# Two closing barriers moved from the end of a log-sum-exp kernel to its beginning

## Chip, cores, metric

One core of a Trainium2 chip. The metric is device time in microseconds (us) of one execution, median of several. All executions quoted here are fast, at a granted clock of 1.00. In the profile DVE is VectorE, ACT ScalarE, POOL GpSimd, SP SyncE and PE TensorE; a q behind a name is that engine's sequencer, and L196 is line 196 of the kernel. The span runs from the program's first instruction to its last.

## The reference

```python
x: float32 [32, 512, 1024], axis = -1
x_max = np.max(x, axis=axis, keepdims=True)
return x_max.squeeze(axis) + np.log(np.sum(np.exp(x - x_max), axis=axis))
```

The kernel reads 67.1 MB, writes 64 KB, and takes the exponentials without subtracting the maximum.

## The kernel before

The 16,384 rows lie as 128 partitions of 128 rows of 1024 numbers. SyncE issues 17 loads of 1 to 16 rows a partition into a ring of 51 rows; ScalarE takes exponentials (and some sums), VectorE the other sums, ScalarE the logarithms, SyncE stores. The parts that matter here:

```python
hook = nc.pop_inst_callback()            # the helper stops recording: what follows is placed by hand
...
body = nc.main_func.blocks[-1]
...
load(0)
n_early = len(body.instructions)         # load 0: will be put ahead of the opening barrier
nc.scalar.preload_act_table_set("natural_log_exp_and_others")
for i, (r, n_dve, parts, by_halves) in enumerate(CHUNKS):
    if i:
        load(i)                          # waits, from load 4 on, for ring rows to be free
    ...                                  # wait for landed[i], exponentials, sums
take_logs(late_row, NB, late[:, : NB - late_row], dves, acts)
nc.sync.wait_ge(act_done, acts)
nc.sync.dma_start(out=out_v, in_=res).then_inc(stored, 16)
nc.sync.sem_clear(range(used[0], used[-1] + 1))
...                                      # load 0 ahead of the opening barrier, the rest right behind it
tc.close()                               # emits the two closing barriers (all five engines)
tc.compile()
nc.sync.wait_ge(stored, 16)              # the program ends when the store has landed
nc.sync.sem_inc(stored, -16)
```

A barrier here works like this in the instruction records: each of the other four engines counts up a semaphore and waits; GpSimd waits for all four counts and then releases the four. The opening barrier stands ahead of the kernel's own code, the two closing ones behind it.

The softmax here doesn't subtract the row's maximum and nothing guards it: scores larger than these inputs give would overflow.

## Time and profile before

| kernel before | |
|---|---|
| time, first 3 runs | 162.74 us (162.58 to 162.85) |
| span of the profiled run | 161.2 us |
| DMA queue, share of 16 engines | 97.3% |
| DVE / ACT busy | 75% / 71% |
| first load issued / landed | 0.00 / 7.6 us |
| second load issued / landed | 0.78 / 25.8 us |
| last load landed / store issued / store landed | 158.2 / 159.6 / 161.2 us |

The timed figure is 1.3 us longer than the span; the runtime's own closing rounds lie behind the span in the semaphore records. The profile's lines stand in the prediction.

### The profile page before, as it was taken

The page shows a single profiled execution, that of the slowest core. Times are in us where ns is not written, and L with a number is a line of the kernel's source. Part 1 is how long each engine was busy: PE and PEld are TensorE (multiplying, and loading weights), DVE is VectorE, ACT ScalarE, POOL GpSimd, SP SyncE. Part 2 cuts the span into 40 slices and gives each one's busy share as a digit, 9 for nine tenths or more (in the row PEclk, how much of TensorE's full clock was granted, in tenths as well). Part 3 has the DMA queues.
Part 4 walks back from the last instruction along what each step waited for, and adds up shares of the span by engine and source line. Part 5 has one row for each costly group of instructions (what it writes and reads, how often), then busy time and mean ns, then how long its engine had stood idle before and what let it go on. Part 6 is the DMA issues. An engine that isn't in the chain of part 4 may idle for free.

```text
span 161.2 us, 149 instructions
## 1 busy us (share of the span) xinstructions
DVE 121.0 (75%) x46; ACT 115.1 (71%) x40; POOL 0.2 (0%) x4
## 2 busy tenths in 40 slices
DVE  0028000003999999999999699999999999999892
ACT  3170005996079960999419993999199999999995
POOL 0000000000000000000000000000000000000000
DMA  7999799999999999999979999999899999999991
GB/s 248 516 488 442 320 457 520 390 390 520 390 390 520 390 390 520 390 390 520 407 342 455 455 455 439 423 423 423 376 439 439 427 448 403 432 415 421 410 409 34
DMA packets 2592, 67.18 MB, mean 417 GB/s; under 512 B 288, under 2 KB 416, under 8 KB 928
## 3 DMA queue, kind: packets, MB, share of 16 engines
q1 hardware_dynamic: 2592, 67.18, 97.3%
HBM read 67.11 MB, written 0.07 MB: 417 GB/s over the span
## 4 chain that ended last, share of the span: by engine, by line
DMA 49%; DVE 29%; ACT 20%; issue 0%
DMA ring<-in_x_dram 49%; DVE sums L154 29%; ACT ring L134 17%; ACT ring L161 3%; ACT res L105 0%
## 5 line engine op out<-in xcount | busy, mean ns | idle before, releaser
L154 DVE TENSOR_REDUCE sums<-ring 128x8 f32<-128x8192 f32 (+5 forms) x14 | 111.2, 7994 | 37.1 <-ACT ring L134 37.0
L134 ACT ACTIVATE ring<-ring 128x8192 f32<-128x8192 f32 (+6 forms) x18 | 104.4, 5835 | 43.7 <-DMA ring<-in_x_dram 43.6
L141 DVE CUSTOM_DVE_ANT_0 ring<-ring 128x512 f32<-128x512 f32 x16 | 9.9, 687 | 0.0
L161 ACT ACTIVATE ring<-ring 128x1024 f32<-128x1024 f32 x9 | 9.3, 1041 | 0.0
L119 ACT ACT_TABLE_LOAD x1 | 1.3, 1283 | 0.8 <-PEq L215 0.8
L161 ACT ACTIVATION_READ_ACCUMULATOR ring<-ring 128x1 f32 x9 | 1.6, 173 | 0.0
L141 DVE DVE_READ_ACCUMULATOR2_ANT sums<- 128x1 f32 x16 | 1.3, 83 | 0.0
L105 ACT ACTIVATE res<-sums 128x81 f32<-128x81 f32 (+1 forms) x2 | 0.5, 246 | 0.0
L105 ACT ACTIVATE res<-late 128x4 f32<-128x4 f32 x1 | 0.2, 173 | 0.0
L215 POOL MEMSET const-bfloat16-1.0<- 128x1 bf16 x1 | 0.1, 102 | 0.0
L215 POOL MEMSET const-uint8-127<- 128x1 uint8 x1 | 0.1, 102 | 0.0
L215 POOL MEMSET const-float32-0.0<- 128x1 f32 x1 | 0.1, 99 | 0.2 <-issue 0.2
L215 POOL MEMSET const-float32-1.0<- 128x1 f32 x1 | 0.1, 99 | 0.0
## 6 DMA issues: line engine op xcount, KB each, us to landing
ring<-in_x_dram SPq DMA_DIRECT2D x1, 7680.0 KB, 25.0
ring<-in_x_dram SPq DMA_DIRECT2D x1, 7168.0 KB, 28.6
ring<-in_x_dram SPq DMA_DIRECT2D x1, 6656.0 KB, 35.7
ring<-in_x_dram SPq DMA_DIRECT2D x1, 4608.0 KB, 20.2
ring<-in_x_dram SPq DMA_DIRECT2D x2, 2048.0 KB, 16.2
ring<-in_x_dram SPq DMA_DIRECT2D x1, 3584.0 KB, 28.3
ring<-in_x_dram SPq DMA_DIRECT2D x1, 2560.0 KB, 27.3
ring<-in_x_dram SPq DMA_DIRECT2D x4, 512.0 KB, 27.0
```

The source lines that it names most:

```text
L105: nc.scalar.activation(out=res[:, lo:hi], in_=src, func=Ln).then_inc(act_done, 1)
L119: nc.scalar.preload_act_table_set("natural_log_exp_and_others")
L134: nc.scalar.activation(out=ring[:, s + lo : s + hi], in_=ring[:, s + lo : s + hi], func=Exp).then_inc(act_done, 1)
L141: nc.vector.tensor_tensor_reduce(out=ring[:, s + j, : D // 2], in0=ring[:, s + j, : D // 2], in1=ring[:, s + j, D // 2 :], scale=1.0, scal ...
L154: nc.vector.reduce_sum(out=sums[:, row + lo : row + hi], in_=ring[:, s + lo : s + hi], axis=AX).then_inc(dve_done, 1)
L161: nc.scalar.activation(out=ring[:, s + j], in_=ring[:, s + j], func=Exp, accum_out=total(row + j),).then_inc(act_done, 1)
L215: nc = _bacc.Bacc("TRN2", target_bir_lowering=False, num_devices=1)
```

## The change

Its intent is to take the two barriers off the end, where they follow the work, and put them at the beginning, where the first load is already under way. The helper is closed at once, so that its barriers are the first thing in the body; all the work comes behind them, and SyncE's wait for the store is the last instruction.

```diff
-    hook = nc.pop_inst_callback()
+    tc.close()
+    tc.compile()
     symbolic, nc._always_lower_symbolic_ap = nc._always_lower_symbolic_ap, False
...
     body = nc.main_func.blocks[-1]
-    assert not body.instructions
+    n_barrier = len(body.instructions)
     load(0)
...
     nc.sync.sem_clear(range(used[0], used[-1] + 1))
+    nc.sync.wait_ge(stored, 16)
+    nc.sync.sem_inc(stored, -16)
...
-    first.instructions = head + work[n_early:] + tail
-    body.instructions = []
+    first.instructions = head
+    body.instructions = work[:n_barrier] + work[n_early:]
...
-    tc.close()
-    tc.compile()
-    nc.sync.wait_ge(stored, 16)
-    nc.sync.sem_inc(stored, -16)
```

More of the change, by code (lines that the diff above doesn't have):

```diff
@@ L176 @@
     nc.sync.sem_clear(range(used[0], used[-1] + 1))
+    nc.sync.wait_ge(stored, 16)
+    nc.sync.sem_inc(stored, -16)
     first = nc.main_func.blocks[0]
     head, work = first.instructions, body.instructions
-    end = next(k for k, i in enumerate(head) if i.opcode == "UnconditionalBranch")
-    head, tail = head[:end], head[end:]
-    for ins in work[:n_early]:
+    for ins in work[n_barrier:n_early]:
         at = next(
@@ L187 @@
         head.insert(at, ins)
-    first.instructions = head + work[n_early:] + tail
-    body.instructions = []
+    first.instructions = head
+    body.instructions = work[:n_barrier] + work[n_early:]
     nc._always_lower_symbolic_ap = symbolic
-    nc.push_inst_callback(hook)
-    tc.close()
-    tc.compile()
-    nc.sync.wait_ge(stored, 16)
-    nc.sync.sem_inc(stored, -16)
 _INS = ['x', 'axis']
```

## The prediction

> **What bounds the kernel now.** I first read the slices of the span for the limit, then the chain that ended last, then the two ends of the span, because the change touches only those. The page of the kernel before:
>
> ```profile
> span 161.2 us, 149 instructions
> DVE 121.0 (75%) x46; ACT 115.1 (71%) x40; POOL 0.2 (0%) x4
> ...
> DMA  7999799999999999999979999999899999999991
> ...
> q1 hardware_dynamic: 2592, 67.18, 97.3%
> ...
> DMA 49%; DVE 29%; ACT 20%; issue 0%
> ```
>
> No compute engine is full (DVE 75%, ACT 71%), while the DMA row is at nine tenths or more nearly everywhere and the one queue's packets take 97.3% of the sixteen engines' span. The chain names DVE and ACT too, since a load waits there for a ring slot, but the DMA row shows that the queue still had bytes meanwhile. So the time is: when the first packets start, plus 67.11 MB at the granted rate, plus what follows the last landing. The busy times by stretch of the kernel before (start:end, span, DVE busy, ACT busy, POOL busy, clock, DMA share, GB/s):
>
> ```profile
> 0.00:1.00 1.00, 0.00 (x0) 0.22 (x1) 0.20 (x4) 1.00 0.00 0
> 1.00:7.00 6.00, 0.00 (x0) 1.06 (x1) 0.00 (x0) 1.00 1.23 483
> 7.00:55.00 48.00, 20.56 (x3) 26.43 (x4) 0.00 (x0) 1.00 1.00 431
> 55.00:157.70 102.70, 100.05 (x44) 85.48 (x31) 0.00 (x0) 1.00 0.99 424
> 157.70:159.60 1.90, 0.34 (x2) 1.85 (x6) 0.00 (x0) 1.00 0.00 0
> ```
>
> Nothing moves in the first microsecond, the engines are full from 1.0 to 157.7, and 3.5 us are left for the tail. (A share over 1 comes of overlapping packets at start-up.)
>
> The start, from the timeline (start, duration, instruction):
>
> ```profile
> 0.00 2.51 SPq L97 DMA_DIRECT2D ring<-in_x_dram  x4
> ...
> 0.78 1.28 ACT L119 ACT_TABLE_LOAD   x1 [0.78 <-PEq L215]
> 7.63 3.62 ACT L134 ACTIVATE ring<-ring 128x4096 f32<-128x4096 f32 x1 [5.57 <-DMA ring<-in_x_dram]
> ```
>
> The first load is issued at 0.00, ahead of the opening barrier. The second, by the chain, is issued at 0.78, right behind it. ScalarE has its table by 2.06 and then stands 5.57 us until the first load lands at 7.6.
>
> The tail, from the timeline, from the waits of the DMA-issuing queue, and from the store's line:
>
> ```profile
> 159.41 0.17 ACT L105 ACTIVATE res<-late 128x4 f32<-128x4 f32 x1
> 159.61 0.35 SPq L173 DMA_DIRECT2D out_dram<-res  x1
> ```
> ```profile
> SPq L198 <- SPq L198: 0.5, 1, 0.5
> SPq L196 <- PEq L196: 0.4, 2, 0.3
> ```
> ```profile
> DMA to landing us min/median/max: 1.6/1.6/1.6
> ```
>
> The store leaves at 159.61 and takes 1.6 us to land: 161.2, the end of the span. The closing barriers (L196) stand inside those 1.6 us. After the second of them SyncE still stands 0.5 us at L198, its wait for the store. That 0.5 us is the line that decides this case: the barriers are over before the store is.
>
> **What the Trainium skill says.** (1) "Perfetto Trace Analysis", section "Per-instruction lifecycle": the reported window of a DMA issued by SyncE ends when its descriptors are made, the movement lies outside it, and the final semaphore write waits for the data write, which can be surprisingly long where the target is HBM. The trace agrees: the store's window is 0.35 us, its landing 1.6 us, for 64 KB. (2) "DMA: Bandwidth & Descriptors", section "Queues, rings and completion order": on each DMA engine the descriptors are consumed in ring order. The packet records agree: the first load's 128 packets of 16 KB start between 1.0 and 6.65, and the first packet of the second load, issued at 0.78, starts only at 6.49. (3) "Runtime: NRT & Kernel Launch", section "The launch sequence": the runtime puts a barrier over all engines of its own behind the kernel, so taking the kernel's own away from the end does not end the program sooner than its last engine. The semaphore records show such a round behind the span. (4) The same page, "Instruction fetch mechanics": a taken branch to an unfetched page stalls. In the trace GpSimd goes from the opening barrier into the closing one, across that branch, in 64 ns (from 0.676 to 0.740), the same 64 ns as between the two closing barriers, so here the branch costs nothing visible.
>
> **The change part by part.**
>
> Removed from the tail: two barriers between the store's issue and SyncE's wait. The semaphore clear starts at 160.0 and takes 0.064; SyncE leaves the second barrier at 160.7 (160.695 in the instruction records). So the pair takes 160.70 - 160.07 = 0.62 us of SyncE. In parallel the store lands at 161.16 (last of its sixteen increments) and the wait goes through at 161.18. Without the barriers SyncE arrives at the wait at about 160.1 and stands there 1.1 us in place of 0.5. Gain on the path: 0.00. The store itself does not move: it waits for ScalarE's last logarithm, and nothing of the barriers stands ahead of it.
>
> Added at the start: the same pair, between the opening barrier's release at 0.70 and the second load's issue. The same 0.62 us, as GpSimd gathers and releases in the same way: second load at 0.78 + 0.62 = 1.40, the third at 1.16 + 0.62 = 1.78, the fourth at 2.6, the table load at 1.40 to 2.68. Does any of these bind? The first load, still ahead of everything, is 4 rows = 2.10 MB, or eight 16 KB packets for each engine. They start from 1.0 on and land by 7.6. At 1.0 us from issue to first packet (the first load: 0.00 to 1.0) the second load's packets can start at 2.4, and no engine comes free for them before 6.49. Slack 4.1 us against 0.62. The table is ready at 2.68, 4.9 us before the first data. The compute engines wait for the same landings as before. Cost on the path: 0.00.
>
> Later loads are issued on DVE's progress, which follows the landings: unchanged. The extra instructions are none: the barriers are the same ones.
>
> Sum: 162.74 - 0.00 + 0.00 = 162.7 us.
>
> **The rivals.**
>
> A. The tail is shortened by the pair: 162.74 - 0.62 = 162.1. For it: the barriers stand behind the work and end only at 160.7. Against it: the 0.5 us wait behind them; they lie wholly in the store's shadow.
>
> B. The start is lengthened by the pair: 162.74 + 0.62 = 163.4. For it: SyncE's first stretch is on the chain (the chain's first transfer begins at 0.78, the second load's issue). Against it: the landing of that load, 25.0 us after issue, is queue time. Loads one and two are 9.96 MB, which take 23 us at 431 GB/s, so its landing is set by the bytes ahead of it and the start at 1.0. The chain's first step is a queue, not an issue latency.
>
> C. A fetch stall at the branch or a longer first stretch on SyncE, of some 2 us: the second load at 3.4, its packets at 4.4, still before 6.49. Nothing: 162.7.
>
> D. A small effect in what is timed outside the span. The timed run that was profiled is 162.53 and its span 161.2, so 1.33 us lie outside. Four engines now stand at the runtime's barrier early. Its round waits for SyncE, which arrives at the same time as before, so I give this at most 0.1 us either way. Start-up may change by as much too: the first packets take about 1.2 us in place of 0.61 while SyncE is making the next loads' descriptors, and that making now comes later.
>
> **Range and chances.** The centre is the sum, 162.7. Repeats before span 162.58 to 162.85, so one median is good to about 0.15. With D's 0.1 and another chip or hour, I allow 0.45 to each side: 162.25 to 163.15, which leaves A and B just outside. Two per cent is 3.25 us, five times the whole pair, so even if A or B held the verdict would be the same: 98% within, 1% on each side, for what I have not thought of (a stall over 4 us at the start on the one side, a removed cost outside the trace on the other).
>
> **What would show it.** Right: the L196 rows lie at 0.7 to 1.4 and none near the end; the second load is issued near 1.40; the first landing stays at 7.6 and the second near 25.8; the store's line still gives 1.6 us; SyncE's last wait grows from 0.5 to about 1.1; the span stays at 161.2 within 0.3. Wrong: a first landing or DMA start that moved by over 0.3 us; a hole in the DMA row near 6 to 7 us; a store whose landing time shrank; or equal spans with timed runs that differ, which would put the cause outside the span.

## The result, and the profile after

| | before | after |
|---|---|---|
| time, median of 6 | 162.79 us (162.41 to 162.95) | 162.62 us (162.52 to 162.84) |
| ratio of fast runs | | 0.9995 (0.9982 to 1.0009) |
| span of the profiled run | 161.2 us | 161.2 us |

A ratio is the mean time of one kernel's fast runs over that of the other's in the same rounds, so not quite the ratio of the medians. The page of the kernel after:

```profile
span 161.2 us, 149 instructions
...
DMA  7999699899899899899889999999899999999990
...
q1 hardware_dynamic: 2592, 67.18, 97.2%
```

The instructions are as many and the queue as full as before. The rows of the line that now makes the barriers (engine, operation, count, durations in ns, first and last start):

```profile
L70 SPq DRAIN  x3: 7/7/7, 0.8 to 1.1; - x3
L70 SPq EVENT_SEMAPHORE  x2: 17/17/17, 1.0 to 1.4; - x2
```

SyncE is in the barriers from 0.8 to 1.4, and none of them is left at the end. The timeline at the start:

```profile
0.00 2.75 SPq L100 DMA_DIRECT2D ring<-in_x_dram  x4
...
1.44 1.28 ACT L122 ACT_TABLE_LOAD   x1 [1.44 <-PEq L70]
7.39 3.62 ACT L137 ACTIVATE ring<-ring 128x4096 f32<-128x4096 f32 x1 [4.66 <-DMA ring<-in_x_dram]
```

The chain that ended last, first before and then after (start, duration, what):

```profile
0.72 0.07 issue
0.78 25.02 DMA ring<-in_x_dram
25.80 0.02 issue
```
```profile
1.37 0.06 issue
1.43 24.36 DMA ring<-in_x_dram
25.80 0.02 issue
```

This pair carries the start: the second load is issued 0.65 us later and lands at the same 25.80. (That the figures are equal is chance: in the eight kernels with this load issued by 1.75 us it landed between 25.43 and 25.80.) All of the delay is taken out of the time it stood in the queue. At the other end, the waits of the issuing queue after:

```profile
SPq L176 <- ACT res L108: 29.1, 1, 29.1
SPq L181 <- SPq L181: 1.1, 1, 1.1
SPq L70 <- PEq L70: 0.5, 2, 0.3
```

The last wait (L181, for the store) has grown from 0.5 to 1.1 us: what the barriers no longer take is now waited for. The store lands about as long after its issue as before (1.55 us before, 1.54 after, by the records), as its line says after:

```profile
DMA to landing us min/median/max: 1.5/1.5/1.5
```

### The profile page after: what moved, and what is told of

Read it like the earlier page. It is cut to its first block, busy times and chain, and to the rows that moved or that the text cites. A ratio compares the mean times of both kernels' runs of the same rounds, so it can differ in the third digit from the quotient of the medians.

```text
span 161.2 us, 149 instructions
## 1 busy us (share of the span) xinstructions
DVE 121.0 (75%) x46; ACT 115.1 (71%) x40; POOL 0.2 (0%) x4
## 2 busy tenths in 40 slices
DMA packets 2592, 67.18 MB, mean 417 GB/s; under 512 B 288, under 2 KB 416, under 8 KB 928
## 3 DMA queue, kind: packets, MB, share of 16 engines
q1 hardware_dynamic: 2592, 67.18, 97.2%
## 4 chain that ended last, share of the span: by engine, by line
DMA 48%; DVE 29%; ACT 20%; issue 0%
DMA ring<-in_x_dram 48%; DVE sums L157 29%; ACT ring L137 17%; ACT ring L164 3%; ACT res L108 0%
```

## The experiments

Equal times say that the sum is nil, not that each part is. The theory to be tested, called the shadow theory: a barrier pair costs nothing at the tail because the store is still on its way, and nothing at the start because the first load still fills the DMA engines. Its rival, the cancelling theory: the pair was worth its 0.62 us at the tail and costs it again at the start. Then the question is how deep each shadow is. All kernels below gave correct results. Kernels are compared only within the same rounds. The runs of the kernel before: 162.61 us (11 runs), 162.59 (11), 162.66 (7). "Packet records" and "semaphore records" are tables of the trace behind the views: the start, duration and size of each piece that the DMA engines moved, and the time of each semaphore update. Descriptors are the orders that SyncE has made for these engines when it issues a load.

### No closing barriers

```diff
# from the kernel after
-    body.instructions = work[:n_barrier] + work[n_early:]
+    body.instructions = work[n_early:]
```

> The kernel after without its two closing barriers anywhere. Shadow theory (the pair costs nothing at either end): 162.7 us, ratio to before 0.998 to 1.001, span 161.2; second load issued at about 0.78 again and the last wait about 1.1 us. Cancelling theory (the pair was worth 0.62 us at the tail and costs 0.62 us at the start, so that moving it nets nothing): 162.1 us, ratio 0.996, span 160.6.

Measured: 162.45 us (162.25 to 162.97), ratio 1.000 (0.998 to 1.002), span 161.2. The chain and the issuing queue's waits:

```profile
0.77 24.93 DMA ring<-in_x_dram
```
```profile
SPq L181 <- SPq L181: 1.1, 1, 1.1
```

The kernel without the pair is no faster than the one with it at the tail. The cancelling theory asked for 162.1 and a ratio of 0.996, outside the interval. It falls: the pair was worth nothing.

### A pair at each end

```diff
# from the kernel before
     n_early = len(body.instructions)
+    for _ in range(2):
+        nc.all_engine_barrier()
```

> The kernel before with a second pair of barriers behind the opening one: a pair at each end. Shadow theory: 162.7 us, ratio 0.999 to 1.002, span 161.2; second load issued at 1.40 to 1.45, first landing near 7.4 as in the kernel after, the last wait 0.5 us as before. Cancelling theory: 163.4 us, ratio 1.004, span 161.8.

Measured: 162.86 us (162.74 to 163.20), ratio 1.0023 (1.0006 to 1.0040): between the two theories, with an interval that reaches the cancelling one's 1.004. The spans decide here and not the times. Those of its six runs are 160.9 to 161.4, those of before 160.9 to 161.6. So nothing was added inside the program. The difference of time and span is 1.76 to 1.84 us in all six, against 1.3 in the kernel before: about 0.5 us came in outside the span. The semaphore records of the profiled run show it in one step of the runtime's last round behind the program, 0.51 us in place of 0.10. The chain and the last wait agree with the shadow theory:

```profile
1.42 24.26 DMA ring<-in_x_dram
25.68 0.02 issue
```
```profile
SPq L200 <- SPq L200: 0.4, 1, 0.4
```

### One barrier more with the pair at each end

```diff
# from the kernel before
     n_early = len(body.instructions)
+    for _ in range(3):
+        nc.all_engine_barrier()
```

> The kernel before with three barriers behind the opening one and its closing pair at the end: one barrier more than the run with a pair at each end, which had 1.8 us between time and span in place of 1.3, all of it in the last round of the runtime's barrier behind the span. If that 0.5 us comes of where the runtime's instructions fall behind the program's, it changes again with one barrier more and may be 1.3 as well as 1.8; if it is a cost of having barriers at both ends, it is 1.8 or more, time 162.9. In both cases the span is 160.9 to 161.6 as before.

Measured: 163.03 us (162.74 to 163.38), ratio 1.0031 (1.0014 to 1.0047); spans 160.8 to 161.3, the shortest of all; time minus span 1.94 to 2.16. So the added time lies outside the span again and is larger, as the reading "a cost of barriers at both ends" had it. It is not shown that this reading is right: the next experiment has the same effect with nothing added at the start. Nor is it the same place: the runtime's last round ends only 0.15 us later than in the kernel before (1.60 in place of 1.45 us after the span), and the rest of the added 0.8 us lies behind it. A rival that no run tests is instruction fetch in the runtime's part: this trace has a fetch 2.04 us after the end of the span. The pair at each end and the three at the tail have no such fetch and were longer all the same.

### Three barriers at the tail

```diff
# from the kernel before
     tc.compile()
+    nc.all_engine_barrier()
     nc.sync.wait_ge(stored, 16)
```

> The kernel before with three closing barriers in place of two, all behind the store. Shadow theory: SyncE leaves the third 0.33 us later than the second, and its last wait shrinks from 0.5 to 0.1 or 0.2 us; span 161.0 to 161.6 as before, time minus span 1.3 to 1.8. If tail barriers were exposed: span 161.5 or more at the same last landing of the store, and a last wait of still 0.5.

Measured: 163.02 us (162.87 to 163.34), ratio 1.0031 (1.0008 to 1.0053), spans 160.9 to 161.4, time minus span 1.92 to 1.97, above the 1.8 that I had allowed. The waits:

```profile
SPq L196 <- PEq L196: 0.4, 2, 0.3
SPq L197 <- PEq L197: 0.3, 1, 0.3
...
SPq L199 <- SPq L199: 0.2, 1, 0.2
```

Inside the span it is as the shadow theory says: the third barrier's 0.33 us is taken from the last wait (0.5 to 0.2) and the span stays. But there is a second, shallower shadow that I had not reckoned with. The runtime's round behind the program passes the four other engines before SyncE. Its semaphore records, relative to the end of the span, put the step just ahead of SyncE's at +0.06 us in the kernel before, at +0.39 here (0.33 later, like the third barrier), and at -1.40 in the kernel after. SyncE's own step stands at 0.13, 0.42 and 0.14. A step takes 0.02 to 0.03 us there, so in the kernel before the other engines were early by only about 0.05 us (an estimate from these figures: 0.13 - 0.06 - 0.02), and a third barrier makes them late. The round then ends at 1.78 in place of 1.45. That accounts for some 0.33 of the 0.6 us added outside the span; the other 0.3 lies behind the round's last step, and no record explains it.

### Eight barriers at the tail

```diff
# from the kernel before
     tc.compile()
+    for _ in range(6):
+        nc.all_engine_barrier()
     nc.sync.wait_ge(stored, 16)
```

> The kernel before with eight closing barriers in place of two, all between the store's issue and the wait for it. One barrier takes 0.328 us of SyncE (from 160.35 to 160.68), so the eighth is left at 160.367 + 7 x 0.328 = 162.66, 1.5 us after the store has landed. Shadow theory: the first 0.5 us of the added 1.97 are hidden, the rest is not: span 162.7, time 164.3 us, ratio 1.009; the last wait 0.0. A theory in which tail barriers cost nothing at all, however many: 162.8. One in which each costs its full 0.328: 164.8, ratio 1.012.

Measured: 164.33 us (164.29 to 164.90), ratio 1.011 (1.009 to 1.013). The three runs without the profile had spans of 162.7 to 162.8, as the shadow theory had it to 0.1 us; full cost would have made 161.2 + 1.97 = 163.2. The spans decide this too: the ratio's interval holds the 1.012 of full cost. That the time (164.29 to 164.36) also fits to 0.1 us is partly luck, since the expectation started from 162.8 us and the kernel before took 162.61 in this call: 0.2 to 0.3 us came in outside the span (time minus span 1.54 to 1.60). (The profiled run was 0.6 us longer: its last load landed 0.34 us late, and VectorE left the last barrier 0.3 us behind the other engines.) The waits:

```profile
SPq L198 <- PEq L198: 1.6, 6, 0.3
SPq L196 <- PEq L196: 0.4, 2, 0.3
```

No wait for the store (L200) is left in this view: the store had landed long before SyncE came. This is what barriers look like once they stick out of the shadow.

### Twenty-four and twelve barriers at the start

```diff
# from the kernel after
     n_early = len(body.instructions)
+    for _ in range(22):          # 10 in the second kernel
+        nc.all_engine_barrier()
```

> The kernel after with 24 barriers behind the opening one in place of two. The k-th is left at 1.046 + 0.328 (k - 1), so the second load is issued at 8.65 in place of 1.43, and its packets can start at about 9.65; the DMA engines run dry of the first load at 6.5 to 7.0. Shadow theory: a hole of about 3 us in the DMA row and a span longer by about that: 164.2, time 165.6 us (165.0 to 166.0), ratio 1.017. Each barrier exposed in full: 22 x 0.328 = 7.2 us, 169.9 us, ratio 1.044. Start barriers never on the path: 162.7.

> The kernel after with 12 barriers behind the opening one in place of two, inside the slack. The twelfth is left at 1.046 + 11 x 0.328 = 4.65, the second load issued at 4.72 (up to 0.4 later if an instruction fetch falls into it, as one barrier of 0.73 us did in the run with 24), its packets possible from 5.7 to 6.1, before the engines are through with the first load at 6.4 to 7.2. Shadow theory: span 161.0 to 161.6, second landing 25.7 to 25.8, time 162.7 us (163.2 if the time outside the span grows by 0.5 as in the run with a pair at each end). Each start barrier exposed: 162.7 + 10 x 0.328 = 166.0 us.

Measured, 24: 167.37 us (167.28 to 167.53), ratio 1.030, span 165.8, some 1.8 us more than I expected. Measured, 12: 163.78 us (163.57 to 164.11), ratio 1.008 (1.006 to 1.010), span 162.3, where I expected no cost at all. The DMA row and chain of the run with 24:

```profile
DMA  7569998998899899889979999999999999999990
```
```profile
9.07 0.06 issue
9.13 21.34 DMA ring<-in_x_dram
30.47 0.02 issue
```

The hole in the second and third slices is the exposed start, and the landing moved from 25.80 to 30.47, 4.67 us, which is the loss of span (161.19 to 165.85 in the trace). By the packet records, the last DMA engine began the second load at 11.06 in place of 7.02 (+4.0), and the first packet of each took about 2.6 to 3.1 us in place of 2.27 (+0.6). In my estimate of 3 us were missing this slow first packet, one barrier that took 0.73 us because GpSimd came to it late (left at 8.07), and the last engine, which counts, not the mean. I had put that barrier down to an instruction fetch, and the expectation for twelve barriers repeats it; but the fetch's packet starts at 8.42, after that barrier was over, so why GpSimd was late is not shown. The chain of the run with 12:

```profile
4.72 0.06 issue
4.78 22.16 DMA ring<-in_x_dram
26.93 0.02 issue
```

The second load is issued 1.6 us before the first engine is free (6.37), yet it lands 1.1 us late. Its first packets took up to 3.2 us, and the last engine began at 7.64. The slack of 4.1 us, which took 1.0 us from issue to packet, is refuted.

### Eight and ten barriers, and the loads apart

```diff
# from the kernel after
     n_early = len(body.instructions)
+    for _ in range(6):           # 8 in the second kernel, 10 in the third
+        nc.all_engine_barrier()
# the third kernel only
+    load(1)
+    for _ in range(6):
+        nc.all_engine_barrier()
...
-        if i:
+        if i > 1:
             load(i)
```

> Eight barriers at the start: left at 1.046 + 7 x 0.328 = 3.34, second load issued at 3.41 (3.45 with the 0.04 that some barriers took more). In the run with twelve (issue 4.78) the last engine began the second load at 7.64, 2.86 us after issue, and packets begun before took up to 3.2 us in place of 2.27, so the lead a load needs is more like 2.9 us than my 1.0. Fixed-lead theory: a lead of 2.9 us fits from 3.41 to 6.3, no cost: span 160.9 to 161.6, 162.6 us. If the lead needed is longer or every 0.33 us at the start costs something: span over 161.7.

> Ten barriers: second load issued at 4.07 to 4.12. Fixed-lead theory: 4.1 + 2.9 = 7.0, against 6.99 at which the last engine is done with the first load in the run with twelve, so about the edge: some slow first packets, span 161.2 to 161.8, between the runs with eight and twelve.

> As the run with twelve barriers, but six more barriers between the second load's issue (4.78) and the third's (about 6.8), which isn't needed before 25 us. If the late and slow first packets in the run with twelve come of SyncE making the descriptors of three loads at once, so that the second load's arrive late, they are gone: second landing 25.7 to 26.1, span 161.0 to 161.5. If they are a fixed lead of a load by itself: second landing 26.9 and span 162.3 again.

The span is that of the profiled run, the time the median of all.

| kernel | second load issued | landed | time, us | span |
|---|---|---|---|---|
| after | 1.43 | 25.80 | 162.62 | 161.2 |
| three barriers at the start (and a pair at the tail) | 1.75 | 25.43 | 163.03 | 160.8 |
| 8 at the start | 3.42 | 25.50 | 162.97 | 161.7 |
| 10 at the start | 4.09 | 26.65 | 163.95 | 162.8 |
| 12 at the start | 4.78 | 26.93 | 163.78 | 162.3 |
| 12, the later loads apart | 4.77 | 26.67 | 163.92 | 162.2 |
| 24 at the start | 9.13 | 30.47 | 167.37 | 165.8 |

The edge lies between an issue at 3.42 and one at 4.09: 2.9 and 2.4 us ahead of the first free engine. Up to it the landing stays within its scatter; behind it, the first packets are slow (2.76 to 3.55 us with ten barriers) and the landing jumps by about 1 us at once. So the fixed-lead theory missed ten barriers, for which it had a span of 161.2 to 161.8. The packets show the beginning earlier: with eight barriers 11 of the 16 first packets took 2.29 to 2.61 us, while none is slow in the kernels with an issue by 1.75. The third kernel rules out that the second load's descriptors are held up by SyncE's work on the two next loads: the third load was issued 2.4 us after the second there, in place of 0.4, and the landing is as late. (That work lay at 7.1 to 8.0 us, beside the first packets; with 12 barriers it was over at 6.05, before them. They are slow in both.) Why the first packets become slow is not settled.

The kernel with eight has a ratio of 1.0021 (1.0006 to 1.0036) and a span 0.3 to 0.5 longer although its second load is in time. Its page and its chain:

```profile
DMA packets 2594, 67.19 MB, mean 416 GB/s; under 512 B 288, under 2 KB 416, under 8 KB 928
...
q1 hardware_dynamic: 2592, 67.18, 96.9%
q14 instruction: 2, 0.02, 0.0%
```
```profile
3.42 22.08 DMA ring<-in_x_dram
25.50 0.02 issue
...
122.41 28.70 DMA ring<-in_x_dram
151.11 0.02 issue
```

There are 2594 packets and only 2592 are the queue's: the other two are fetches of instructions, of 8 KB, which the kernel before has only ahead of its span. One of them is at 149.6, and the load of three rows that landed at 150.64 before lands at 151.11. The packet records support the fetch as the cause. In these experiments eight fetches fall where data are moving (with 8, 10, 12 and 24 barriers and with the loads apart; the one at 8.42 falls into the hole of the run with 24); right at the end of each a data packet starts, and it takes 0.38 to 0.66 us more than others of its size. So one DMA engine loses 0.7 to 1.0 us. (Some packets are 0.3 to 0.5 us slow with no fetch beside them, two of them in the kernel after.) The run with ten has the same step in the same load: it lands 4.43 us after the load ahead of it, in place of 3.68, with a fetch at 148.5. So of the 1.6 us that ten barriers add to the span, about 0.75 are this and only 0.85 the start. The run with 12 has two fetches (132.8 and 147.4) and no such step. Its engines were spread over 1.8 us at the end of the second load and those with eight over 0.6, so one engine could lose a microsecond there without being the last; that is argued and not tested.

Apart from this step, the span follows the second landing. In ten of the thirteen profiled runs the span ends 135.4 to 135.7 us after the second landing; the others are 8 and 10 barriers at the start (136.1 to 136.2, the step just told) and eight at the tail.

### The kernel after once more

No edit.

> The kernel after once more, beside the others on the same chip. Shadow theory: ratio to before 0.998 to 1.002, time minus span 1.3, span 160.9 to 161.6.

Measured: 162.43 us (162.31 to 162.61), ratio 0.9994 (0.998 to 1.001), time minus span 1.31 to 1.38, spans 161.0 to 161.3. The equality is repeated in other rounds.

## Why the prediction was right

It said 162.7 us; the median is 162.62, within the range.

**The bound.** Right. The queue is at 97% in both kernels, and the stretches at its two ends are as long.

**The tail: gain 0.00.** Right and shown, by the last wait (0.5 to 1.1), by the kernel without any pair (ratio 1.000), and by eight barriers, whose span sticks out by what was calculated. What I missed is that the wait of SyncE is not the only measure: the other engines were only about 0.05 us early at the runtime's barrier, not 0.5.

**The start: cost 0.00.** Right. Second load at 1.43 (1.40 predicted), table at 1.44, landing at 25.80 as before. Two of its readings were not right, and neither bears on the result. The 23 us for the first two loads give a landing at 1.0 + 23.1 = 24.1 and not 25.8: in the packet records the engines finish the second load between 24.60 and 25.50 (the first packets took about 1.2 us in place of 0.61, and the sixteen engines end 0.9 us apart), and its last semaphore update comes 0.3 us later. And the share over 1 in the window 1 to 7 us is not shown to come of overlap: the view counts each packet in full where it starts, so the second load's packets begun before 7 us count with what they moved afterwards; cut at 7 us the share is 0.95.

**The slack of 4.1 us.** Wrong in size. The term is "at 1.0 us from issue to first packet". That 1.0 us was of a load into idle engines. A load that is to follow a running one without a later landing had to be issued between 2.4 and 2.9 us ahead of the first free engine. Measured from the issue at 1.43, the slack is 2.0 to 2.7 us, half to two thirds of the estimate. The pair's 0.65 us fits into it three times, so the result did not depend on it. Rival C, a delay to 3.4 us, would still have been hidden, as the landing in the run with eight barriers shows at 3.42, but closer to the edge than I thought.

**The first landing "stays at 7.6".** It came at 7.39. That is within the scatter: 7.59 and 7.40 us in two kernels with the second load at 0.77 and 0.79, 7.58 and 7.38 in two with it at 1.42. Rival D's idea that later descriptor work changes the start-up has weak support over all the kernels: the median of the 16 first packets was 1.08 to 1.23 us in the four with the second load at 0.8, 1.05 to 1.17 in the four with it at 1.4 to 1.8, and 0.86 to 1.02 in the five with it later. That is a correlation, and it doesn't reach the span. Its other half, a change outside the span of at most 0.1 us, holds for this pair of kernels (1.3 in both).

**Rivals A and B.** Each excluded by the chain and the last wait, and their cancelling by the kernel without barriers.

## What to carry to other kernels

Before moving a fixed cost off an end, look at what is in flight beside it: here a store of 1.6 us covered the tail barriers and a first load of 7 us covers them at the start, so that moving, removing or doubling the pair leaves the span alone. A shadow has a depth, and more than one engine may stand in it: measure it by adding the cost until it shows, as the estimate of the slack at the start was one and a half to two times what was measured. When a time moves and the span doesn't, look at what lies behind the program before explaining it from inside.

## What the Trainium skill lacked or had wrong

- "DMA: Bandwidth & Descriptors", section "Latency and other measured facts", gives about 600 ns to the first byte for a DMA of this kind. Here the first packet came 1.0 us after issue into idle engines.
- No page has the lead that a load needs to follow another without loss: between 2.4 and 2.9 us here, judged by the landing. With less, the first packets of 60 KB took up to 3.55 us in place of 2.27, and the load landed about 1 us late.
- "Runtime: NRT & Kernel Launch", section "The launch sequence", has the runtime's closing barrier, but nothing by which a program's last instructions change the time behind it: the time outside the span was 1.29 to 1.39 us in the kernels before and after, and 1.5 to 2.2 us in the four with barriers added to the kernel before, in part unexplained.
- The same page, section "Instruction fetch mechanics", calls the cost of a fetch mostly hidden and speaks of 16 KiB blocks. The packet records show single fetches of 8 KB on the DMA engines that move the data: a data packet starts right at the end of each of the eight that fell where data were moving and takes 0.38 to 0.66 us more than its like, and with eight barriers at the start the span grew by 0.3 to 0.5 us.
- No page has the cost of a kernel's own barrier over five engines: 0.33 us each when they follow one another.
